# Gate table of a PEER layer from one float32r product a token, with 20 down blocks ahead of the up stage

## The chip, the cores and the metric

One core of one Trainium2 chip runs the whole program. The metric is device time in microseconds, lower is better; the median over several executions is compared.

## What is computed

One transformer block on 256 tokens of width 2048, in float32: an adaptive norm driven by a vector `c` (six vectors of 2048 come out of `silu(c) @ ada_w`), a hybrid mixer (sparse attention beside a gated recurrence), a second adaptive norm, and a PEER feed-forward layer. The sixth vector, `gt2`, scales the feed-forward output at the very end. The change lies in the PEER layer:

```python
def peer_ffn(h, wq, keys, down, up):
    q = (hf @ wq).reshape(T, PEER_HEADS, 2, PEER_DQ // 2)
    s = jnp.einsum('thpd,hpkd->thpk', q, keys)
    v1, i1 = lax.top_k(s[:, :, 0], PEER_TOPK)
    v2, i2 = lax.top_k(s[:, :, 1], PEER_TOPK)
    ...
    cidx = (i1[..., :, None] * PEER_KEYS + i2[..., None, :])
    vals, pick = lax.top_k(cand, PEER_TOPK)
    eidx = jnp.take_along_axis(cidx, pick, axis=-1)
    g = jax.nn.softmax(vals, axis=-1)
    ...
    act = gelu(einsum('td,thkd->thk', x_c, down[e_c])) * g_c
    out = einsum('thk,thkd->td', act, up[e_c])
```

`cand` holds the 256 sums of `v1` and `v2`. There are 16384 experts, and each token picks 8 heads x 16 = 128 of them; the result is scaled by `gt2` and added to `x`.

## The kernel before

The PEER layer is computed densely: all 16384 experts are applied to all 256 tokens, and the activations are multiplied by a table of gates that is zero where an expert wasn't picked. The stages, in order of time:

- **wq** (from 477 us): four blocks of queries and key scores, and the searches for the 16 best (VectorE).
- **down**: 32 down blocks `d` of 512 experts, `gelu(down @ h)` with experts on partitions and tokens along the free axis. `turned` (L376) makes one: eight weight subblocks of 128x1024, 24 matmuls of 256 columns each. The first `LAG` = 14 blocks run ahead of the up stage; their results are stored to `xd` in DRAM and loaded again (`xS`) when they are due.
- **up**: 16 groups of four up blocks `u`, 48 matmuls of 512 columns each, added to `acc` by VectorE. From `LAG` on, a down block runs ahead of every two up blocks (groups 6 to 14); earlier groups hold up blocks alone.

All these products are float32 in three passes: every weight tile `raw` (1 MB, loaded through SP's queue into four buffers, in the order of the list `items`) is split into a high and a low float32r part, `wh` by a ScalarE cast (L206) and `wl` by a VectorE subtraction (L207); `fill` keeps two subblocks ready ahead of TensorE.

The **gate table** needs, for each token, a 128x128 matrix with the gates at the picked pairs of keys. `picks` (L1130, once for each half of the tokens) turns the search results into key indices and gates, transposes them (`pkT`) and copies them to `idT` and `gT` (picks along partitions, tokens along the free axis). `w_build` (L1178) then takes steps of four tokens. In step q VectorE makes the one-hot rows `oh` of both key indices (L1185), ScalarE scales the one-hot rows of the first by the gates of step q-1 (L1206), TensorE multiplies for step q-2 in plain float32 (L1201), and ScalarE copies the product of step q-3 from PSUM into `stg` (L1193); every eight steps POOL's queue stores `stg` to `wd` in DRAM. There are 64 steps. `act` (L1231) later loads the table's part `wt`, multiplies it into the activations and splits them (`ah`, `al`).

Such side work is written as generators. `tick` runs once a weight subblock and advances the first generator in the list of jobs by `RATES[prio]` steps: evictions have priority 0, searches and `act` 1, `picks` 2, `w_build` 3; while `w_build` is at step `WK` or below it goes at the full rate (two steps a subblock in the down stage). So `RATES` and `WK` set how thickly the table's steps lie among the down matmuls. All jobs that are left are run without a pause ahead of the last of the `LAG` blocks. Weight splits have a raised priority in the scheduler, so they are placed ahead of the steps.

The sixth vector's 16 chunks `ada` of 1 MB come in the same list `items`, one behind each up block of groups 4 to 7; VectorE reduces each against `cb` (L228, 128x2048). At the end of group 8 the vector is closed and broadcast into `cb` (`bcast_row`).

Of the kernel before, what the change touches and what calls it, by code (L numbers as in the profile page):

```python
# [7 lines left out]
F32 = mybir.dt.float32  # L8
F32R = mybir.dt.float32r
U32 = mybir.dt.uint32  # L10
I32 = mybir.dt.int32
AF = mybir.ActivationFunctionType
OP = mybir.AluOpType
AX = mybir.AxisListType

P = 128
D = 2048
S = 256
# [9 lines left out]
NE = 16384  # L28
NEB = NE // 512
NUG = NE // 1024  # L30
LAG = 14
RATES = (2, 1.8, 1, 1.1)
WK = 4
RG = 2
CDS = ((0, 1, 16), (1, 4, 8), (4, 16, 4))
NCD = 88
# [9 lines left out]
AHEAD = 2  # L46

TURN, WROOM, XTURN = 24, 1088, 8
LEAD = 50
LEAD2 = 350  # L50
SEGS = (('f', 0, 2), ('a', 0, 4), ('f', 2, 6), ('a', 4, 8))
# [16 lines left out]
def kernel(  # L68
# [24 lines left out]
    V, A, T, G = nc.vector, nc.scalar, nc.tensor, nc.gpsimd  # L93
# [12 lines left out]
    def ps_t(name):  # L106
        return ps[0].tile([P, 512], F32, tag="t", bufs=ps[2], name=name)
# [25 lines left out]
    x1d = dp.tile([NT, P, D], F32, name="x1d")  # L133
    xd = dp.tile([LAG, P, 4, S], F32, name="xd")
    wd = dp.tile([8, P, P, 32], F32, name="wd")


    items = []
# [11 lines left out]
    for ch in STREAM.replace(" ", ""):  # L150
# [6 lines left out]
        else:  # L157
            src, o = wid[ch].pop(0)
# [6 lines left out]
    for j in range(4):  # L165
        for h in range(2):
            add_w(wq[j, h], shift=TURN)
    for e in range(LAG):
        for h in range(2):
            add_w(down[e, h], shift=TURN)  # L170
    for g in range(NUG):
        for o in range(2):
            e = 2 * g + 2 + o
            if LAG <= e < NEB:
                for h in range(2):
                    add_w(down[e, h], shift=TURN)
            for q in range(2):
                add_w(up[g, 2 * o + q])
                if 4 <= g < 8:
                    items.append(("ada", 4 * (g - 4) + 2 * o + q))  # L180

    pos = {"load": 0, "take": 0, "sub": 0, "lead": 0, "end": 0, "n": 0, "adl": 0}
    raws, avs = [], []
# [258 lines left out]
    ea, e0, eq = ExitStack(), ExitStack(), ExitStack()  # L442
# [61 lines left out]
    for which, i0, i1 in SEGS:  # L504
# [11 lines left out]
        if not sums[which]:  # L516
            if which == "f":
                t = [vp.tile([P, 2, NT, 512], F32, tag="av", bufs=ADAB, name=f"part{i}") for i in range(2)]
                sums["f"] = [[t[b // 2][:, b % 2, tb] for tb in range(NT)] for b in range(4)]
            else:  # L520
                t = sqp.tile([P, 4, NT, 512], F32, name="sums")
# [534 lines left out]
    for i in range(8):  # L1056
        t = x1T[:, 2 * i:2 * i + 2]
# [19 lines left out]
    kq = e4.enter_context(tc.tile_pool(name="kq", bufs=1))  # L1077
    idT = kq.tile([P, S, 2], F32, name="idT")
    gT = kq.tile([P, S], F32, name="gT")
# [50 lines left out]
    def picks(tb):  # L1130

        hi = kq.tile([P, 2, PH, TOPK], U32, tag="hi", bufs=1, name=f"hi{tb}")
        hf = kq.tile([P, 2, PH, TOPK], F32, tag="hf", bufs=1, name=f"hf{tb}")
        mf = kq.tile([P, 16, TOPK], F32, tag="mf", bufs=1, name=f"mf{tb}")
        sel = kq.tile([P, 3, PH, TOPK], F32, tag="sel", bufs=1, name=f"sel{tb}")
        V.tensor_copy(mf, mi[:, tb])

        V.tensor_scalar(hi[:, 0], pk[:, tb], 3, None, OP.logical_shift_right)
        V.tensor_scalar(hi[:, 1], pk[:, tb], 2, None, OP.logical_shift_right)
        V.tensor_copy(hf, hi)  # L1140
        ra, rb = hf[:, 0], hf[:, 1]
        V.tensor_scalar(ra, ra, -1.0, 0.0, OP.add, OP.max)
        V.scalar_tensor_tensor(out=ra, in0=rb, scalar=-6.0, in1=ra, op0=OP.add, op1=OP.max)
        ex = sel[:, 2]
        V.tensor_scalar(rb, ra, 8.0, 8.0, OP.mult, OP.add)
        V.scalar_tensor_tensor(out=rb, in0=ra, scalar=16.0, in1=rb, op0=OP.mult, op1=OP.min)
        V.tensor_scalar(ex, ra, 4.0, 24.0, OP.mult, OP.add)
        V.tensor_tensor(rb, rb, ex, OP.min)
        V.tensor_copy(ex, pk[:, tb])
        V.tensor_tensor(rb, ex, rb, OP.subtract)  # L1150
        V.tensor_tensor(ex, vl[:, tb], vl[:, tb, :, 0:1].to_broadcast([P, PH, TOPK]), OP.subtract)
        A.activation(ex, ex, AF.Exp)
        yield
        m4 = mf.rearrange("p (h o) k -> p h o k", o=2)
        hp = PH // 2
        shape = [P, hp, TOPK, TOPK]
        io = iota[:, 0:16].unsqueeze(1).unsqueeze(1).to_broadcast(shape)
        for o in range(2):
            for hh in range(2):
                hs = slice(hp * hh, hp * (hh + 1))  # L1160
                eq = kq.tile(shape, F32, tag="eq", bufs=3, name=f"eq{tb}{o}{hh}")
                V.tensor_tensor(eq, hf[:, o, hs].unsqueeze(3).to_broadcast(shape), io, OP.is_equal)
                V.tensor_tensor(eq, eq, m4[:, hs, o].unsqueeze(2).to_broadcast(shape), OP.mult)
                yield
                V.tensor_reduce(sel[:, o, hs], eq, AX.X, OP.add)
        s8 = kq.tile([P, PH], F32, tag="s8", bufs=1, name=f"s8{tb}")
        V.tensor_reduce(s8, ex, AX.X, OP.add)
        V.reciprocal(s8, s8)
        V.tensor_tensor(ex, ex, s8.unsqueeze(2).to_broadcast([P, PH, TOPK]), OP.mult)
        yield  # L1170
        tp = ps_t(f"pkT{tb}")
        for i in range(3):
            T.transpose(tp[:, i * P:(i + 1) * P], sel[:, i].rearrange("p h k -> p (h k)"), ident)
        yield
        A.copy(idT[:, tbs[tb]].rearrange("p t i -> p i t"), tp[:, 0:2 * P].rearrange("p (i t) -> p i t", i=2))
        A.copy(gT[:, tbs[tb]], tp[:, 2 * P:3 * P])

    def w_build():  # L1178

        stg, ohs, gas, wps = {}, {}, {}, {}  # L1180
        for q in range(64 + 3):
            wn[0] = q
            if q < 64:
                oh = kq.tile([P, 4, 2, P], F32, tag="eq", bufs=3, name=f"oh{q}")
                V.tensor_tensor(oh, iota.unsqueeze(1).unsqueeze(1).to_broadcast([P, 4, 2, P]),  # L1185
                                idT[:, 4 * q:4 * q + 4].unsqueeze(3).to_broadcast([P, 4, 2, P]), OP.is_equal)
                ohs[q] = oh
            if 0 <= q - 3:
                p_, tg = q - 3, (q - 3) // 8
                if p_ % 8 == 0:  # L1190
                    stg[tg] = kq.tile([P, P, 32], F32, tag="stg", bufs=1, name=f"stg{tg}")
                o = (p_ % 8) * 4
                A.copy(stg[tg][:, :, o:o + 4], wps.pop(p_).rearrange("p (k i) -> p i k", k=4))  # L1193
                if p_ % 8 == 7:
                    G.dma_start(wd[tg], stg.pop(tg))
            if 0 <= q - 2 < 64:
                p_ = q - 2
                oh = ohs.pop(p_)
                wps[p_] = (ps_p if p_ % 2 else ps_t)(f"w{p_}")
                for k in range(4):  # L1200
                    T.matmul(wps[p_][:, k * P:(k + 1) * P], oh[:, k, 1], oh[:, k, 0], start=True, stop=True)  # L1201
            if 0 <= q - 1 < 64:
                p_ = q - 1
                for k in range(4):
                    t = 4 * p_ + k
                    A.activation(ohs[p_][:, k, 0], ohs[p_][:, k, 0], AF.Copy, scale=gT[:, t:t + 1])  # L1206
            yield


# [85 lines left out]
    for g in range(NUG):  # L1295
        for o in range(2):
# [7 lines left out]
            for q in range(2 * o, 2 * o + 2):  # L1304
# [10 lines left out]
                if q % 2 == 0 and LAG <= eb < NEB:  # L1315
                    finish(0)
                    add(act(eb, upp), 1)
        if g == NUG // 2:
            ada_close(5, 0, NDC)
            add(bcast_row(cb, 5), 1)  # L1320
        if g < NUG - 1:
# [96 lines left out]
```

## Time and profile before

| what | value |
|---|---|
| median of three runs | 2052.03 us (2051.98 to 2058.9) |
| profiled execution, device time | 2056.6 us |
| its span, first to last instruction | 2054.8 us |
| TensorE matmul busy | 1979.6 us (96%) |
| VectorE busy | 1451.0 us (71%) |
| ScalarE busy | 1016.1 us (49%) |
| DMA | 509.12 MB, 248 GB/s mean |

The profile is of one execution. Busy time is the union of an engine's instructions; TensorE's matmuls overlap one another in the records, so the time from one start to the next, and not a record's length, is what a matmul costs. PEld is TensorE's weight load, which runs beside the matmuls. A table of stretches gives start:end and length in us, then for each engine its busy us and the count of its instructions, then TensorE's granted clock (1.00 is full speed), the busy share of the DMA engines and GB/s. A group names the source line, the engine and the tiles as output<-inputs; a releaser is what ended an engine's idle time.

### The profile page before, as it was taken

To read this page: it belongs to the slowest core of one execution; us is meant where nothing else is said; L and a number is where in the kernel's file an instruction comes from. 1 tells how busy PE (TensorE), PEld (TensorE's weight loads), DVE (VectorE), ACT (ScalarE), POOL (GpSimd) and SP (SyncE) were. 2 spreads that over 40 slices of the span, in tenths; PEclk is the share of its full clock that TensorE was granted. 3 is DMA by queue.
4 is the path that set the end of the run, shared out by engine and by line. 5 is a ranking of instruction groups with operands and counts; after the bars stand their busy time and mean duration, and the time that the engine had idled before them with its cause. 6 is when DMAs were issued, how large, how long until landed. Compare 5 with 4: busy or idle time off the path is not lost.

```text
span 2054.8 us, 31264 instructions
## 1 busy us (share of the span) xinstructions
PE 1979.6 (96%) x12602; PEld 1751.4 (85%) x12602; DVE 1451.0 (71%) x2149; ACT 1016.1 (49%) x1454; POOL 61.0 (3%) x95
## 2 busy tenths in 40 slices
PE   5999998998999999999999999999999999999998
PEld 4777565788999999998888789899999889999997
DVE  7888999887999666546667766665555555555566
ACT  2544676455446988645444334444444444444442
POOL 0000000000000000001000000000000000000000
PEclk8999998898999999999999999999999999999999
DMA  9898778995455666778767777776555666556663
GB/s 361 333 361 337 273 302 326 343 342 207 165 179 192 227 244 244 253 262 308 256 232 259 270 263 258 256 265 209 197 199 200 214 203 208 202 203 207 198 226 130
DMA packets 75873, 509.12 MB, mean 248 GB/s; under 512 B 8528, under 2 KB 9040, under 8 KB 20176
## 3 DMA queue, kind: packets, MB, share of 16 engines
q1 hardware_dynamic: 63792, 450.50, 60.7%
q0 software_dynamic: 11936, 56.63, 8.2%
q8 instruction: 98, 1.61, 0.3%
q14 instruction: 47, 0.39, 0.1%
HBM read 478.78 MB, written 28.31 MB: 247 GB/s over the span
## 4 chain that ended last, share of the span: by engine, by line
PE 64%; issue 16%; DVE 12%; DMA 4%; ACT 2%; POOL 1%; DVEq 0%; SPq 0%; POOLq 0%; ACTq 0%
PE d L374 8%; PE d L373 8%; PE d L372 8%; PE u L356 7%; PE u L355 7%; PE u L357 7%; DVE wl L207 3%; DVE av L228 3%; DMA raw<-in_ada_w_dram 2%; PE wq L372 2%; PE wq L373 2%; PE wq L374 2%; PE y L357 1%; PE y L355 1%; PE y L356 1%
## 5 line engine op out<-in xcount | busy, mean ns | idle before, releaser
L207 DVE TENSOR_TENSOR wl<-raw,wh 128x1024 fp32r<-128x1024 f32 x649 | 788.9, 1221 | 462.8 <-ACT wh L206 460.0
L206 ACT CAST wh<-raw 128x1024 fp32r<-128x1024 f32 x649 | 679.9, 1050 | 808.7 <-PE u L357 374.2
L372 PE MATMUL d<-xH,wh 128*128 128x256 f32 x2048 | 571.4, 279 | 0.0
L374 PE MATMUL d<-xH,wl 128*128 128x256 f32 x2048 | 568.0, 277 | 0.8 <-DVE wl L207 0.7
L373 PE MATMUL d<-xL,wh 128*128 128x256 f32 x2048 | 567.6, 277 | 0.0
L356 PE MATMUL u<-wl,ah 128*128 128x512 f32 x1024 | 400.0, 391 | 4.2 <-DVE wl L207 4.2
L355 PE MATMUL u<-wh,ah 128*128 128x512 f32 x1024 | 398.9, 390 | 0.0
L357 PE MATMUL u<-wh,al 128*128 128x512 f32 x1024 | 398.6, 389 | 0.0
L374 PEld LDWEIGHTS d<-xH,wl 128*128 128x128 f32 x2048 | 384.9, 188 | 1.3 <-DVE wl L207 1.2
L372 PEld LDWEIGHTS d<-xH,wh 128*128 128x128 f32 x2048 | 385.2, 188 | 0.7
L373 PEld LDWEIGHTS d<-xL,wh 128*128 128x128 f32 x2048 | 384.9, 188 | 0.7
L356 PEld LDWEIGHTS u<-wl,ah 128*128 128x128 f32 x1024 | 192.2, 188 | 46.4 <-DVE wl L207 7.4
L357 PEld LDWEIGHTS u<-wh,al 128*128 128x128 f32 x1024 | 192.4, 188 | 40.2
L355 PEld LDWEIGHTS u<-wh,ah 128*128 128x128 f32 x1024 | 192.2, 188 | 39.7
L228 DVE SCALAR_TENSOR_TENSOR av<-av,cb 128x2048 f32<-128x2048 f32 x64 | 145.8, 2283 | 6.2 <-DMA av<-in_ada_w_dram 6.2
L1185 DVE TENSOR_TENSOR oh<-con,idT 128x1024 f32<-128x1024 f32 x64 | 78.0, 1223 | 58.4 <-PE w L1201 58.4
L1206 ACT ACTIVATE oh<-oh,gT 128x128 f32<-128x128 f32 x256 | 83.1, 396 | 24.9 <-DVE oh L1185 24.9
L372 PE MATMUL wq<-xH,wh 128*128 128x256 f32 x256 | 73.5, 288 | 2.5 <-ACT xH L206 2.5
L373 PE MATMUL wq<-xL,wh 128*128 128x256 f32 x256 | 73.2, 286 | 0.0
L374 PE MATMUL wq<-xH,wl 128*128 128x256 f32 x256 | 73.0, 285 | 0.0
L1262 DVE TENSOR_TENSOR acc<-acc,u 128x512 f32<-128x512 f32 x112 | 71.5, 679 | 0.0
L1201 PE MATMUL w<-oh 128*128 128x128 f32 x512 | 69.8, 276 | 0.2 <-ACT stg L1193 0.2
(359 smaller groups left out, 2007.9 us busy)
## 6 DMA issues: line engine op xcount, KB each, us to landing
raw<-in_down_dram SPq DMA_DIRECT2D x128, 1024.0 KB, 5.2
raw<-in_up_dram SPq DMA_DIRECT2D x128, 1024.0 KB, 5.1
av<-in_ada_w_dram SPq DMA_DIRECT2D x64, 1024.0 KB, 7.0
raw<-in_w_a_dram SPq DMA_DIRECT2D x32, 1024.0 KB, 9.0
raw<-in_ada_p_dram SPq DMA_DIRECT2D x16, 1024.0 KB, 7.1
raw<-in_w_out_dram SPq DMA_DIRECT2D x16, 1024.0 KB, 7.9
raw<-in_wq_dram SPq DMA_DIRECT2D x16, 1024.0 KB, 5.2
wd<-stg POOLq DMA_DIRECT2D x8, 2048.0 KB, 8.0
```

What stands on the lines that cost most here:

```text
L206: A.copy(dst_h, src)
L207: V.tensor_tensor(dst_l, src, dst_h.bitcast(F32), OP.subtract)
L228: V.scalar_tensor_tensor(out=t, in0=t, scalar=1.0, in1=cb, op0=OP.mult, op1=OP.mult, accum_out=m)
L355: T.matmul(o, ah, bh, start=first, stop=False)
L356: T.matmul(o, ah, bl, start=False, stop=False)
L357: T.matmul(o, al, bh, start=False, stop=last)
L372: T.matmul(o, wh[:, kk, ws], bH[:, kc], start=f and i % 2 == 0, stop=False)
L373: T.matmul(o, wh[:, kk, ws], bL[:, kc], start=False, stop=False)
L374: T.matmul(o, wl[:, kk, ws], bH[:, kc], start=False, stop=e and i % 2 == 1)
L1185: V.tensor_tensor(oh, iota.unsqueeze(1).unsqueeze(1).to_broadcast([P, 4, 2, P]), idT[:, 4 * q:4 * q + 4].unsqueeze(3).to_broadcast([P, 4, ...
L1206: A.activation(ohs[p_][:, k, 0], ohs[p_][:, k, 0], AF.Copy, scale=gT[:, t:t + 1])
L1262: V.tensor_tensor(a, a, pst[tb], OP.add)
```

## The change

- The table's product: the gate `gT` is split once into `gh` (float32r) and `gl` (the rest). In each step VectorE makes the one-hots as float32r, ScalarE writes the first one-hot times `gh` and VectorE the first one-hot times `gl` into a new tile `ga`, and one float32r matmul of 256 columns per token gives both parts. The two parts go to two PSUM tiles of two tokens each; ScalarE copies the high part to `stg` and VectorE adds the low part. The pipeline of steps is one longer (product for step q-3, copies for step q-4).
- `oh` and `ga` get tags of their own with three buffers each, `ga` with an offset of 48 elements inside its tile (`GPLACE`); the tag `eq` remains with `picks`.
- `LAG` 14 to 20: 20 down blocks ahead of the up stage; 20 stores and loads of `xd`; groups 0 to 8 hold up blocks alone, 9 to 14 have the down blocks.
- `RATES` for `picks` 1 to 0.7, for `w_build` 1.1 to 0.51; `WK` 4 to 0. `picks` gets one more empty step ahead of its transposes.
- The sixth vector's chunks move from groups 4 to 7 into groups 9 to 12, its end from group 8 to 13.

```diff
@@ -28,9 +28,10 @@
 NE = 16384
 NEB = NE // 512
 NUG = NE // 1024
-LAG = 14
-RATES = (2, 1.8, 1, 1.1)
-WK = 4
+LAG = 20
+RATES = (2, 1.8, 0.7, 0.51)
+WK = 0
+ADG = 9
 RG = 2
 CDS = ((0, 1, 16), (1, 4, 8), (4, 16, 4))
 NCD = 88
@@ -46,6 +47,8 @@
 AHEAD = 2
 
 TURN, WROOM, XTURN = 24, 1088, 8
+
+GPLACE = 48
 LEAD = 50
 LEAD2 = 350
 SEGS = (('f', 0, 2), ('a', 0, 4), ('f', 2, 6), ('a', 4, 8))
@@ -176,8 +179,8 @@
                     add_w(down[e, h], shift=TURN)
             for q in range(2):
                 add_w(up[g, 2 * o + q])
-                if 4 <= g < 8:
-                    items.append(("ada", 4 * (g - 4) + 2 * o + q))
+                if ADG <= g < ADG + 4:
+                    items.append(("ada", 4 * (g - ADG) + 2 * o + q))
 
     pos = {"load": 0, "take": 0, "sub": 0, "lead": 0, "end": 0, "n": 0, "adl": 0}
     raws, avs = [], []
@@ -1168,6 +1171,7 @@
         V.reciprocal(s8, s8)
         V.tensor_tensor(ex, ex, s8.unsqueeze(2).to_broadcast([P, PH, TOPK]), OP.mult)
         yield
+        yield
         tp = ps_t(f"pkT{tb}")
         for i in range(3):
             T.transpose(tp[:, i * P:(i + 1) * P], sel[:, i].rearrange("p h k -> p (h k)"), ident)
@@ -1175,35 +1179,53 @@
         A.copy(idT[:, tbs[tb]].rearrange("p t i -> p i t"), tp[:, 0:2 * P].rearrange("p (i t) -> p i t", i=2))
         A.copy(gT[:, tbs[tb]], tp[:, 2 * P:3 * P])
 
+    def turn_tile(tag, place, dt, name):
+
+        t = kq.tile([P, 4 * 2 * P + (64 if place else 0)], dt, tag=tag, bufs=3, name=name)
+        return t[:, place:place + 4 * 2 * P].rearrange("p (k o i) -> p k o i", k=4, o=2)
+
     def w_build():
 
         stg, ohs, gas, wps = {}, {}, {}, {}
-        for q in range(64 + 3):
+        gl = kq.tile([P, S], F32, name="gl")
+        gh = kq.tile([P, S], F32R, name="gh")
+        A.copy(gh, gT)
+        V.tensor_tensor(gl, gT, gh.bitcast(F32), OP.subtract)
+        for q in range(64 + 4):
             wn[0] = q
             if q < 64:
-                oh = kq.tile([P, 4, 2, P], F32, tag="eq", bufs=3, name=f"oh{q}")
+                oh = turn_tile("oh", 0, F32R, f"oh{q}")
                 V.tensor_tensor(oh, iota.unsqueeze(1).unsqueeze(1).to_broadcast([P, 4, 2, P]),
                                 idT[:, 4 * q:4 * q + 4].unsqueeze(3).to_broadcast([P, 4, 2, P]), OP.is_equal)
                 ohs[q] = oh
-            if 0 <= q - 3:
-                p_, tg = q - 3, (q - 3) // 8
+            if 0 <= q - 4:
+                p_, tg = q - 4, (q - 4) // 8
                 if p_ % 8 == 0:
                     stg[tg] = kq.tile([P, P, 32], F32, tag="stg", bufs=1, name=f"stg{tg}")
                 o = (p_ % 8) * 4
-                A.copy(stg[tg][:, :, o:o + 4], wps.pop(p_).rearrange("p (k i) -> p i k", k=4))
+                for k, w in enumerate(wps.pop(p_)):
+                    w4 = w.rearrange("p (k o i) -> p i o k", k=2, o=2)
+                    d = stg[tg][:, :, o + 2 * k:o + 2 * k + 2]
+                    A.copy(d, w4[:, :, 0])
+                    V.tensor_tensor(d, d, w4[:, :, 1], OP.add)
                 if p_ % 8 == 7:
                     G.dma_start(wd[tg], stg.pop(tg))
-            if 0 <= q - 2 < 64:
-                p_ = q - 2
-                oh = ohs.pop(p_)
-                wps[p_] = (ps_p if p_ % 2 else ps_t)(f"w{p_}")
+            if 0 <= q - 3 < 64:
+                p_ = q - 3
+                oh, ga = ohs.pop(p_), gas.pop(p_)
+                wps[p_] = [ps_t(f"w{p_}0"), (ps_p if p_ % 2 else ps_t)(f"w{p_}1")]
                 for k in range(4):
-                    T.matmul(wps[p_][:, k * P:(k + 1) * P], oh[:, k, 1], oh[:, k, 0], start=True, stop=True)
+                    T.matmul(wps[p_][k // 2][:, k % 2 * S:k % 2 * S + S], oh[:, k, 1], ga[:, k].rearrange("p o i -> p (o i)"),
+                             start=True, stop=True)
             if 0 <= q - 1 < 64:
                 p_ = q - 1
+                ga = turn_tile("ga", GPLACE, F32R, f"ga{p_}")
+                gas[p_] = ga
+                hot = ohs[p_][:, :, 0].bitcast(F32)
+                V.tensor_tensor(ga[:, :, 1], hot, gl[:, 4 * p_:4 * p_ + 4].unsqueeze(2).to_broadcast([P, 4, P]), OP.mult)
                 for k in range(4):
                     t = 4 * p_ + k
-                    A.activation(ohs[p_][:, k, 0], ohs[p_][:, k, 0], AF.Copy, scale=gT[:, t:t + 1])
+                    A.activation(ga[:, k, 0], hot[:, k], AF.Copy, scale=gh[:, t:t + 1].bitcast(F32))
             yield
 
 
@@ -1315,7 +1337,7 @@
                 if q % 2 == 0 and LAG <= eb < NEB:
                     finish(0)
                     add(act(eb, upp), 1)
-        if g == NUG // 2:
+        if g == ADG + 4:
             ada_close(5, 0, NDC)
             add(bcast_row(cb, 5), 1)
         if g < NUG - 1:
```

## Rows read from the trace of the kernel before

**Rows 1.** The page: engines' busy us, share, instructions; TensorE's busy tenths in 40 slices.
```profile
PE 1979.6 (96%) x12602; PEld 1751.4 (85%) x12602; DVE 1451.0 (71%) x2149; ACT 1016.1 (49%) x1454; POOL 61.0 (3%) x95
PE   5999998998999999999999999999999999999998
```

**Rows 2.** Stretches: length; busy us (x count) of PE, PEld, DVE, ACT, POOL; PEclk; DMA.
```profile
576.20:949.50 373.30, 368.26 (x3218) 366.23 (x3217) 260.86 (x345) 248.02 (x474) 18.05 (x31) 1.00 0.65 234
599.00:626.00 27.00, 23.17 (x196) 22.24 (x195) 26.93 (x39) 12.15 (x14) 0.54 (x1) 1.00 0.56 193
715.50:834.50 119.00, 119.00 (x1052) 119.00 (x1050) 78.61 (x67) 96.58 (x213) 4.78 (x9) 1.00 0.65 239
862.40:949.50 87.10, 87.10 (x771) 87.10 (x770) 44.07 (x42) 39.85 (x43) 9.00 (x14) 1.00 0.79 279
526.30:550.70 24.40, 24.40 (x210) 24.40 (x210) 23.35 (x112) 10.57 (x13) 0.00 (x0) 1.00 0.50 172
576.20:655.00 78.80, 73.99 (x638) 72.46 (x636) 78.57 (x187) 38.16 (x47) 1.61 (x3) 1.00 0.56 194
```

**Rows 3.** Stretches, instructions on tile `d` alone: PE, PEld, ACT; PEclk; DMA.
```profile
715.50:834.50 119.00, 95.58 (x769) 90.05 (x769) 4.98 (x9) 1.00 0.65 239
862.40:949.50 87.10, 87.10 (x770) 87.02 (x768) 4.80 (x9) 1.00 0.79 279
```

**Rows 4.** Table of stretches in the up stage; columns as in rows 2.
```profile
1005.80:1136.40 130.60, 130.60 (x578) 108.15 (x576) 88.59 (x102) 56.37 (x54) 8.02 (x11) 1.00 0.71 242
1136.40:1217.10 80.70, 78.06 (x337) 62.54 (x336) 59.42 (x60) 31.39 (x30) 0.00 (x0) 1.00 0.79 287
1217.10:1304.40 87.30, 87.30 (x578) 79.68 (x577) 57.49 (x59) 37.72 (x38) 1.76 (x2) 1.00 0.72 253
1391.60:1435.20 43.60, 43.60 (x289) 39.82 (x288) 24.54 (x26) 18.85 (x19) 0.88 (x1) 1.00 0.61 205
```

**Rows 5.** Stretches, instructions on tile `w` alone: PE, PEld, ACT; PEclk; DMA.
```profile
576.20:949.50 373.30, 69.78 (x512) 63.89 (x512) 36.10 (x64) 1.00 0.65 234
715.50:834.50 119.00, 36.44 (x283) 33.94 (x281) 19.25 (x34) 1.00 0.65 239
```

**Rows 6.** Waits of TensorE, 576 to 949 us: total us, times, longest.
```profile
PE pkT L1173 <- DVE sel L1165: 4.0, 4, 1.8
```

**Rows 7.** Groups by line, 1136.4 to 1217.1 us: busy, mean ns, idle before, releaser.
```profile
L228 DVE SCALAR_TENSOR_TENSOR raw<-raw,cb 128x2048 f32<-128x2048 f32 x6 | 13.8, 2292 | 14.7 <-DMA raw<-in_ada_w_dram 14.7
...
L356 PE MATMUL u<-wl,ah 128*128 128x512 f32 x112 | 44.4, 397 | 2.6 <-DVE wl L207 2.6
```

**Rows 8.** Groups by line over the span; columns as in rows 7.
```profile
L207 DVE TENSOR_TENSOR wl<-raw,wh 128x1024 fp32r<-128x1024 f32 x649 | 788.9, 1221 | 462.8 <-ACT wh L206 460.0 <-PE a L357 2.2
L206 ACT CAST wh<-raw 128x1024 fp32r<-128x1024 f32 x649 | 679.9, 1050 | 808.7 <-PE u L357 374.2 <-PE d L373 290.7 <-PE wq L373 46.5
L1185 DVE TENSOR_TENSOR oh<-con,idT 128x1024 f32<-128x1024 f32 x64 | 78.0, 1223 | 58.4 <-PE w L1201 58.4
L1206 ACT ACTIVATE oh<-oh,gT 128x128 f32<-128x128 f32 x256 | 83.1, 396 | 24.9 <-DVE oh L1185 24.9
L1193 ACT COPY stg<-w 128x512 f32<-128x512 f32 x64 | 36.1, 584 | 4.2 <-DMA wd<-stg 3.0 <-PE w L1201 1.1
L1215 ACT ACTIVATE xT<-d 128x512 f32<-128x512 f32 x64 | 38.0, 593 | 28.4 <-PE d L374 28.4
L1262 DVE TENSOR_TENSOR acc<-acc,u 128x512 f32<-128x512 f32 x112 | 71.5, 679 | 0.0
L1311 DVE TENSOR_TENSOR acc<-acc,xr 128x512 f32<-128x512 f32 x8 | 5.5, 683 | 0.0
L1238 DVE TENSOR_TENSOR xT<-xT,wt 128x256 f32<-128x256 f32 x72 | 27.3, 420 | 8.6 <-ACT xT L1215 8.6
L800 DVE SCALAR_TENSOR_TENSOR pt<-sc,rq,con 128x256 f32<-128x256 f32 x16 | 7.4, 476 | 0.0
```

**Rows 9.** Groups of VectorE by line, 576.2 to 655 us; columns as in rows 7.
```profile
L207 DVE TENSOR_TENSOR wl<-raw,wh 128x1024 fp32r<-128x1024 f32 x27 | 32.5, 1212 | 0.0
```

## The prediction

> **What bounds the kernel now.** I read the page first: TensorE is busy 96% of the span, VectorE, the next, 71% [rows 1]. A busy share alone doesn't say that TensorE runs at its pace, so the second view is a table of stretches with edges at the starts of blocks (a block is the 192 matmuls of one `turned` call or the 48 of one `up_block`). Four clean down blocks take 87.1 us for 770 matmuls, so 21.78 us a block and 113.1 ns a matmul [rows 2, 3]; twelve clean up blocks take 130.6 us, 10.88 us each [rows 4]. [...] So from the down stage on, the time is a count of matmul columns plus the places where a block is longer than its clean length. Those places are what the change touches:
> - The 14 down blocks ahead of the up stage take 373.3 us, and 14 clean ones would take 304.9: 68.4 us over [rows 2].
> - The gate table's products stand in this stage: 512 instructions (two for each of 256 tokens) [rows 5]. In the steady part, 119.0 us hold four down blocks (769 matmuls) and 283 table instructions [rows 2, 3, 5]. 119.0 - 87.1 = 31.9 us for 283 is 112.7 ns each, 0.90 us for a step of four tokens, 57.7 us for all 64 steps. No cover: TensorE is busy for all 119.0 us and nothing waits, so each of these us is on the path.
> - 18 other matmuls of the stage (3218 - 14 x 192 - 512 [rows 2, 5]) are some 2.0 us at the same 113 ns. 68.4 - 57.7 - 2.0 = 8.7 us are true stalls. They lie in the second to fourth block; in the second, the longest but for the table's, VectorE is busy 26.93 of 27.0 us [rows 2] and TensorE waits for `sel` of `picks`, 4.0 us in four waits [rows 6]; part of the rest is weights that came late behind the same work.
> - In the up stage, 80.7 us hold seven up blocks, 76.2 at the clean length: 4.5 us lost [rows 4]. These are the blocks in which the chunks of the sixth vector (1 MB each) are loaded beside weights while no down block runs; VectorE sits 14.7 us waiting for such chunks and TensorE 2.6 us for VectorE's splits behind them [rows 7].
>
> **The table's product.** Now: float32, 128 columns, two instructions, 57.7 us. After: one float32r product of 256 columns with a 128x128 stationary operand, the very shape of the down matmul. 256 x 113.1 ns = 29.0 us. The same shape in the wq blocks costs more: 24.40 us for 192 of it and 18 others [rows 2], (24.40 - 18 x 0.113) / 192 = 116.5 ns, which would make 29.8 us. I take 29.0, since the table's products will stand among the down matmuls. Term: -28.7 us (-27.9 at the dearer pitch). [...]
>
> **What it adds on VectorE and ScalarE.** Prices are of one instruction [rows 8]. VectorE per step: the one-hot table stays at 1.22 us; new are a product of 512 elements (0.68, as the adds of 512) and two adds of 256 out of PSUM. For these 0.42 us is the nearest row in kind (a two-input product of 256), 0.476 the nearest with a PSUM source. So 2.74 to 2.85 us in place of 1.22; I take 2.74. ScalarE: four scalings are unchanged, one copy of 512 (0.58) becomes two of 256, between 0.29 (half) and 0.58 (no shorter) each, so 0 to 0.58 us more. Once: a 256-wide copy and subtraction, below 1 us.
> Following the ticks by hand: `picks` ends in the second eighth of down block 3 (counted from 0), the table runs from the fourth eighth of block 3 to the sixth of block 17, some 114 weight subblocks. VectorE's work there: 114 x 1.221 = 139.2 (splits) and 64 x 2.74 = 175.4, together 314.6 us. TensorE's: 14.25 x 21.78 + 29.0 = 339.4 us. So VectorE fills 93%, with 24.8 us or 0.39 us a step to spare (0.28 at the upper price). ScalarE: 114 x 1.05 + 28 x 0.59 + 64 x (83.1 / 64 = 1.30 for four scalings and 0.58 to 1.17) = 257 to 294 us, 87% at most. At the old rate of some nine steps a block VectorE would need 9.8 + 9 x 2.74 = 34.4 us beside 21.8 + 9 x 0.453 = 25.9 us of TensorE; at the new 4 to 5 it fits. That is the cover for the 97 us (64 x 1.52) that VectorE gains, and if it goes, the excess is on the path.
> The wq blocks show such a cover holding: VectorE busy 23.35 of 24.40 us, 96%, and TensorE busy all of it [rows 2]. `picks` shows it failing at 99.7%. Between them, at 93% with uneven steps (4 or 5 a block, now and then two close together), I put **+4 us** of stalls; bounds 0 and 29 (below).
>
> **Waits that it adds.** The one-hot tile of step q takes the buffer of step q-3, whose product is now emitted in the same step and not in the step before. VectorE already waits there, 58.4 us for 64 steps [rows 8], with nothing lost on TensorE. Behind the waiting instruction are the splits of the next weights, for which TensorE waits; two subblocks (5.4 us) lie ready ahead. Each add waits for a ScalarE copy; behind it stand the same splits. The `stg` tile still has one buffer: the first copy of each eight steps waits for the store to `wd` behind POOL's queue. These transfers, six more stores and loads of `xd` among them, move through POOL's queue, where the gelu's third buffer gives them two blocks of time. No term.
>
> **Picks.** Same VectorE work, 78.57 us busy in 78.8 less 32.5 of splits and 2.4 of one-hot, so 43.7 us of search and picks (two one-hots at 1.22) [rows 2, 9]. Now its last piece falls due in the middle of block 2; after, in block 3, with one more step between the last sums and the transposes that wait for them. By the transposes' new place (576.2 + 3.1 x 21.78 + 1.5 = 645) VectorE owes 43.7 + 26 x 1.22 = 75.4 us of 69: still 6 us short, part of which the extra step and the table's own lead (products stand three steps behind the one-hots) can absorb. Left between 0 and 8.7 us; I take 5, so **-3.7 us**.
>
> **Down blocks and chunks moved.** Six down blocks change place; in the mixed groups one down and two up blocks take 43.6 us [rows 4], the sum of their clean lengths is 43.54: nothing. The sixth vector's 16 chunks pass, in SP's queue, from up-only groups into groups 9 to 12, where each pair of up blocks has a down block beside it. Groups of that mixed kind that carried chunks took 87.3 us for two pairs (one of two such groups stands), against 43.6 for one without [rows 4]: no loss. The weights that now load earlier by those places only gain time. Term **-4.5 us**, bounds -4.5 and 0. The broadcast of that vector moves with it at its own cost.
>
> **Sum.** -28.7 - 3.7 - 4.5 + 4 = -33 us. The profiled execution took 2056.6 us, so 2023.6 for one like it; the median of the runs shown is 2052.0, 4.6 below it, so I predict **2019 us**.
>
> **Rivals.**
> 1. All of it hides: no stall from VectorE, `picks` clean: 2052.0 - 28.7 - 8.7 - 4.5 = 2010. For: 93%. Against: uneven steps, VectorE owing 6 us at the start of the table.
> 2. VectorE becomes the bound: an add of 256 out of PSUM into a strided tile costs twice the row. 64 x 0.84 = 54 us more, less 25 to spare, 29 on the path in place of 4: 2044. For: no row has VectorE reading and writing such strides. Against: the ScalarE copy with the same strides took its usual 0.58 us. [...]
> 3. **Slower**: the in-order waits don't overlap. If VectorE stands at each one-hot for the product of the same step as long as now (58.4 / 64 = 0.91 us) and at each add for its copy (0.29 to 0.58), 1.5 to 2.1 us a step, 64 x 1.8 - 25 = 90 us come on the path: 2052 - 37 + 90 = 2105. It turns slower by over 0.5% from (37 + 25 + 10) / 64 = 1.1 us of wait a step. For: ScalarE is some 80% busy, and its casts stand between the copies. Against: a wait for TensorE shrinks as VectorE falls behind, and now it costs nothing.
> 4. The change doesn't do what it says: the float32r product takes as long as the float32 pair. 2052 - 3.7 - 4.5 + 0 = 2044. Against: the same shape runs at 113 ns beside it.
>
> **How the numbers follow.** A measurement of this kernel can tell 0.5%, 10 us, from no change. Forecast with its stalls of 0 to 15 us (2012 to 2031): 0.54. Rival 1: 0.15. Rival 2, from 2031 to 2050: 0.19, half of it below 2042. Rival 4: 0.03. Rival 3: 0.09, of it 0.01 within 0.5%. Faster: 0.54 + 0.15 + 0.10 = 0.79; same: 0.09 + 0.03 + 0.01 = 0.13; slower 0.08. The range for 8 in 10 runs from rival 1 with 2 us to spare, 2008, to 2042.
>
> **What would show it.** Right: 256 records of the table's product at the down matmul's length; a down block with 4 or 5 steps at 23.6 to 24.0 us; VectorE at 90 to 95% there; groups 4 and 5 at 10.88 us a block; no loss in groups 9 to 12. Wrong: TensorE idle before `d` or the product, released by VectorE's splits or adds, above 10 us in sum; an add above 0.6 us; down blocks above 25 us; VectorE idle for ScalarE's copies by over 1 us a step.

## The result, and the profile after

Measured beside one another, the kernel before has a median of 2053.0 us and the changed one 2027.6 us (2027.1 to 2029.0): a ratio of 0.987, with its interval from 0.985 to 0.989. The forecast was 2019 with a range of 2008 to 2042, so the time lies inside it, 8.6 us above the point. The profiled execution of the changed kernel took 2027.1 us, with a span of 2025.3; its lines have moved (casts and splits of weights L209 and L210, the table's one-hots L1198, scaling L1228, product L1218, copies L1209, adds L1210).

Engines' busy time and TensorE's tenths, from the page, for [rows 1]:

```profile
PE 1953.6 (96%) x12346; PEld 1728.4 (85%) x12346; DVE 1529.3 (76%) x2342; ACT 1024.1 (51%) x1519; POOL 67.6 (3%) x107
...
PE   5999898898999999999999999999999999999998
```

256 instructions of TensorE are gone (12602 to 12346), 26 us of its busy time with them, and VectorE has 78 us more. The stretches, with the columns of [rows 2]; the first is the whole down stage with its 20 blocks:

```profile
574.70:1057.10 482.40, 475.45 (x4113) 473.66 (x4112) 398.19 (x586) 312.56 (x599) 21.24 (x37) 1.00 0.68 240
664.50:1002.60 338.10, 335.58 (x2897) 335.00 (x2896) 280.47 (x358) 241.00 (x509) 11.18 (x21) 1.00 0.67 237
660.00:757.00 97.00, 97.00 (x859) 97.00 (x858) 81.40 (x102) 69.30 (x145) 3.20 (x6) 1.00 0.67 237
760.00:935.00 175.00, 173.08 (x1467) 172.90 (x1468) 144.34 (x184) 123.33 (x261) 5.85 (x11) 1.00 0.67 237
1013.60:1057.10 43.50, 43.50 (x386) 43.50 (x385) 24.47 (x26) 20.85 (x23) 7.92 (x12) 1.00 0.92 339
1102.30:1232.90 130.60, 130.60 (x578) 108.18 (x577) 87.57 (x103) 56.40 (x55) 8.71 (x12) 1.00 0.72 241
1276.40:1385.20 108.80, 108.80 (x482) 90.12 (x481) 72.93 (x86) 46.92 (x45) 6.71 (x9) 1.00 0.71 237
1450.50:1799.40 348.90, 348.90 (x2305) 318.54 (x2304) 229.68 (x234) 150.86 (x152) 7.07 (x8) 1.00 0.74 253
```

- The up stage is clean in these stretches (its third block takes 12.48 us, 12.77 before). Twelve up blocks take 130.60 us, as in [rows 4]; the last row holds all 16 chunks beside eight down and sixteen up blocks and takes 348.9 us, where eight times the clean 43.6 makes 348.8.
- The down stage takes 482.4 us. Less six blocks of 21.78 this is 351.7, against 373.3 for the same 14 blocks and the table before [rows 2]: 21.6 us won.
- Of two stretches of the same make (down blocks with four or five table steps each) the first runs at 97.00 / 859 = 112.9 ns a matmul and the second, by its busy time, at 173.08 / 1467 = 118.0. The clock is 1.00 in both. From start to start in the records it is 113.3 ns until the gap at 759.6 us, 117.8 from there to 937, and 113.35 again. This is the part of the result that the prediction had no term for.

The same on the tile `w` alone, PE, PEld, DVE, ACT, for [rows 5]:

```profile
576.00:1057.00 481.00, 40.62 (x256) 34.43 (x256) 48.26 (x128) 43.61 (x128) 1.00 0.68 241
```

Waits of TensorE in the down stage (total us, times, longest), for [rows 6]:

```profile
PE w L1218 <- DVE stg L1210: 2.5, 3, 1.4
PE pkT L1177 <- DVE sel L1172: 2.2, 2, 1.1
PE pkT L1177 <- DVE sel L1168: 1.4, 1, 1.4
PE d L377 <- DVE wl L210: 0.7, 1, 0.7
```

Groups by line in the down stage, for [rows 8]:

```profile
L210 DVE TENSOR_TENSOR wl<-raw,wh 128x1024 fp32r<-128x1024 f32 x161 | 196.2, 1220 | 40.0 <-ACT wh L209 38.8
...
L1228 ACT ACTIVATE ga<-oh,gh 128x128 fp32r<-128x128 f32 x256 | 83.0, 394 | 18.1 <-DVE oh L1198 16.3
L1198 DVE TENSOR_TENSOR oh<-con,idT 128x1024 fp32r<-128x1024 f32 x64 | 78.1, 1221 | 33.4 <-PE w L1218 33.3
L1210 DVE TENSOR_TENSOR stg<-stg,w 128x256 f32<-128x256 f32 x128 | 48.3, 421 | 10.3 <-ACT stg L1209 10.3
L1225 DVE TENSOR_TENSOR ga<-oh,gl 128x512 fp32r<-128x512 f32 x64 | 43.6, 683 | 0.0
L1209 ACT COPY stg<-w 128x256 f32<-128x256 f32 x128 | 43.6, 400 | 11.6 <-DMA wd<-stg 11.6
L1218 PE MATMUL w<-ga,oh 128*128 128x256 f32 x256 | 40.6, 280 | 2.5 <-DVE stg L1210 2.5
```

The new wait of the table is read along its idle column, from L1209 upwards: ScalarE stands 11.6 us for the store of `stg`, VectorE's adds 10.3 us for ScalarE's copies, and TensorE 2.5 us for the buffer that an add has not yet emptied. One such place, in order of time (start, us, engine and line; idle time before it and its releaser), on ScalarE:

```profile
759.49 0.94 ACT L1209 COPY stg<-w 128x256 f32<-128x256 f32 x3 [2.77 <-DMA wd<-stg]
760.29 1.07 ACT L209 CAST wh<-raw 128x1024 fp32r<-128x1024 f32 x1
```

and on VectorE:

```profile
756.75 0.68 DVE L1225 TENSOR_TENSOR ga<-oh,gl 128x512 fp32r<-128x512 f32 x1
759.91 1.08 DVE L1210 TENSOR_TENSOR stg<-stg,w 128x256 f32<-128x256 f32 x3 [2.48 <-ACT stg L1209]
761.39 1.22 DVE L210 TENSOR_TENSOR wl<-raw,wh 128x1024 fp32r<-128x1024 f32 x1 [0.40 <-ACT wh L209]
```

The `wd` store issued at 748.7 us lets ScalarE go at 759.5. TensorE's stream breaks here (0.9 us from one start to the next), and it is from this break that the matmuls run at 117.8 ns.

### The profile page after: what moved, and what is told of

The parts are those of the page before. It is cut to its first block, busy times and chain, and to the rows that moved or that the text cites. A ratio compares the mean times of both kernels' runs of the same rounds, so it can differ in the third digit from the quotient of the medians.

```text
span 2025.3 us, 30935 instructions
## 1 busy us (share of the span) xinstructions
PE 1953.6 (96%) x12346; PEld 1728.4 (85%) x12346; DVE 1529.3 (76%) x2342; ACT 1024.1 (51%) x1519; POOL 67.6 (3%) x107
## 4 chain that ended last, share of the span: by engine, by line
PE 75%; DVE 10%; issue 10%; DMA 3%; ACT 2%; POOL 1%; SPq 0%; DVEq 0%; POOLq 0%
PE u L359 11%; PE u L358 11%; PE u L360 11%; PE d L377 8%; PE d L376 8%; PE d L375 8%; DVE av L231 3%; DVE wl L210 3%; PE wq L375 2%; PE wq L376 2%; PE wq L377 2%; PE y L360 1%; PE y L358 1%; PE y L359 1%; DMA wd<-stg 1%
## 5 line engine op out<-in xcount | busy, mean ns | idle before, releaser
L210 DVE TENSOR_TENSOR wl<-raw,wh 128x1024 fp32r<-128x1024 f32 x649 | 789.3, 1220 | 374.7 <-ACT wh L209 372.0
L209 ACT CAST wh<-raw 128x1024 fp32r<-128x1024 f32 x649 | 680.2, 1051 | 768.5 <-PE u L360 364.2
L1198 DVE TENSOR_TENSOR oh<-con,idT 128x1024 fp32r<-128x1024 f32 x64 | 78.1, 1221 | 33.4 <-PE w L1218 33.3
L1228 ACT ACTIVATE ga<-oh,gh 128x128 fp32r<-128x128 f32 x256 | 83.0, 394 | 18.1 <-DVE oh L1198 16.3
L1210 DVE TENSOR_TENSOR stg<-stg,w 128x256 f32<-128x256 f32 x128 | 48.3, 421 | 10.3 <-ACT stg L1209 10.3
```

The costliest lines, as they stand in the source:

```text
L209: A.copy(dst_h, src)
L210: V.tensor_tensor(dst_l, src, dst_h.bitcast(F32), OP.subtract)
L1228: A.activation(ga[:, k, 0], hot[:, k], AF.Copy, scale=gh[:, t:t + 1].bitcast(F32))
```

## The experiments

Three questions: which part of the change earns what, what the 117.8 ns come from, and whether a better version follows.

**The parts, one at a time.** The product alone, with `LAG`, rates, `WK`, chunks and the `picks` step as before:

```diff
-LAG = 20
-RATES = (2, 1.8, 0.7, 0.51)
-WK = 0
-ADG = 9
+LAG = 14
+RATES = (2, 1.8, 1, 1.1)
+WK = 4
+ADG = 4
...
-        yield
```

> The new product alone: 14 blocks ahead, the old rates (picks 1, table 1.1, full rate up to step 4), one empty step fewer in picks, the sixth vector's chunks in groups 4 to 7. Theory (VectorE has no room at the old rate): per block some nine steps ask VectorE for 9.8 + 9 x 2.74 = 34.4 us beside 25.8 us of TensorE, so the table stage lasts as long as VectorE's 64 x 2.74 + its splits, some 245 us where it was 213: 20 to 35 us slower than the kernel before, 2073 to 2088 us. Rival (the splits' priority and the three steps of slack absorb it): the product's gain comes through at the old rate as well, 2053 - 29 + 5 = 2029 us.

Measured: 2065.1 us, ratio 1.0051 (1.0035 to 1.0068): slower than before, if less than expected. Two down blocks with nine steps and two with eight to ten, in stretches as above:

```profile
728.10:861.20 133.10, 119.63 (x914) 115.28 (x913) 121.99 (x173) 100.07 (x254) 4.27 (x8) 0.94 0.56 214
```

and TensorE's waits in the table stage:

```profile
PE d L377 <- DVE wl L210: 12.5, 11, 2.5
PE w L1217 <- DVE stg L1209: 5.5, 9, 1.7
```

The four blocks take 33.3 us each (34.4 worked out from VectorE's durations). TensorE idles 13.5 us, released by VectorE, and the clock falls to 0.94 in a stretch where it was 1.00 before. But VectorE too idles, 11 us: no engine is full, they wait for one another in order. The 0.94 is a mean: in four spells, 17.1 us in all, each of which began during a stop of 1.5 to 2.7 us or within 1.5 us of its end, the granted clock is 0.50, the lower of the two levels in the records (1 - 0.5 x 17.1 / 133.1 makes the 0.94). There 69 matmuls take 213 ns from start to start in place of 113 to 118, some 7 us of TensorE's time; how much of it adds to the 10.7 was not separated. So the thin rates are what makes the product pay. The expected times overshot because from the first product to the last the table takes 240 us here and 203 before, but holds 7.8 down blocks in place of 6.6: some 27 of these 37 us are blocks that have to run anyway.

Everything but the product, the float32 pair kept. One place of the product against the changed kernel; the one-hots, scalings and copies of the table are the old ones too:

```diff
-                    T.matmul(wps[p_][k // 2][:, k % 2 * S:k % 2 * S + S], oh[:, k, 1], ga[:, k].rearrange("p o i -> p (o i)"),
-                             start=True, stop=True)
+                    T.matmul(wps[p_][:, k * P:(k + 1) * P], oh[:, k, 1], oh[:, k, 0], start=True, stop=True)
```

> All of the change but the product: the old float32 product with its two instructions, 20 blocks ahead, the new rates, the extra step in picks, the chunks in groups 9 to 12. Theory: the product is worth 28.7 us, the rest of the change some 7 to 9 us (picks 3.6, chunks 4.5), so 2053 - 8 = 2045 us, and no slow stretch as long as no gap opens. Rival (the spreading out is what gained, by leaving VectorE room): most of the 25 us are here, 2032 us or less.

Measured: 2047.9 us, ratio 0.9966 (0.9953 to 0.9978). The sum's terms for `picks` and chunks make -8.2 us, and -6.5 came. Where the table now ends just ahead of the up stage, the second and third up block take 11.84 and 16.29 us, against 10.88 and 12.77 before: 4.5 us lost there. The two parts alone give +10.7 and -6.5 us, together -25.4: the gain is in the pair.

The changed kernel with its chunks back in groups 4 to 7, where with `LAG` 20 all are up-only:

```diff
-ADG = 9
+ADG = 4
```

> The changed kernel with the sixth vector's chunks in groups 4 to 7 again, which now hold up blocks alone. Theory: chunks beside up blocks alone cost 4.5 us for the seven blocks after the start of group 4 in the kernel before; here all four groups are of that kind, so 4.5 to 10 us more: 2032 to 2038 us. Rival (the loss of the kernel before came from the late start of weight loads behind the table, not from the chunks): within 1 us of 2027.6.

Measured: 2046.2 us, ratio 0.9955 (0.9938 to 0.9971), 18.6 us above the changed kernel, far more than expected. Sixteen up blocks with chunks:

```profile
1232.60:1427.10 194.50, 179.58 (x769) 142.75 (x768) 146.25 (x164) 74.98 (x72) 9.64 (x13) 1.00 0.82 295
```

Their waits, on VectorE and on TensorE:

```profile
DVE raw L231 <- DMA raw<-in_ada_w_dram: 36.3, 14, 4.1
```

```profile
PE u L359 <- DVE wl L210: 14.9, 15, 1.6
```

Sixteen clean blocks take 174.1 us, so 20.4 are lost, 1.3 a chunk, where eight chunks before cost 4.5 us or 0.6 each [rows 4, 7]. The DMA share is 0.82 in place of 0.72, VectorE stands for chunks and TensorE behind it for splits. Moving the chunks is therefore not a separate gain of 4.5 us: it belongs to `LAG` 20, which takes 18.6 us more without it.

`picks` at its old rate and without the added step, the rest as changed:

```diff
-RATES = (2, 1.8, 0.7, 0.51)
+RATES = (2, 1.8, 1, 0.51)
...
-        yield
```

> The changed kernel with the picks stage as before: one step a subblock in place of 0.7 and one empty step fewer ahead of its transposes. Theory: TensorE's waits for picks were 5 us in the changed kernel and 8.7 before, so 3 to 4 us more, 2031 us, give or take what the pace behind the gaps makes (up to 4 us in the blocks next to them). Rival (the table's later start is what costs): the earlier start leaves more room and the time is the same or less, 2025 to 2028 us.

Measured: 2037.4 us (2028.9 to 2039.5), ratio 0.9908 (0.9882 to 0.9935). The waits for `sel` are back at 4.0 us in four, as in [rows 6]. The rest is not `picks`: the profiled execution (2039.5) waits 7.1 us for `stg` and runs some 270 us at 117.8 ns, against 191 in the changed kernel.

**The buffer behind the gaps.** Theory: the one `stg` buffer makes the table's gaps, and the gaps make the slow pace. Rival: the pace has its own cause, and two buffers only save 3 us. To make room, the four one-hots of `picks` share a tile with the second buffer:

```diff
-    kt = kq.tile([P, 16, P], F32, tag="stg", bufs=1, name="kt")
+    kt = kq.tile([P, 16, P], F32, tag="stg", bufs=2, name="kt")
+    eqb = kq.tile([P, 4, 1024], F32, tag="stg", bufs=2, name="eqb")
...
-                eq = kq.tile(shape, F32, tag="eq", bufs=3, name=f"eq{tb}{o}{hh}")
+                eq = eqb[:, 2 * o + hh].rearrange("p (h a b) -> p h a b", h=hp, a=TOPK)
...
-                    stg[tg] = kq.tile([P, P, 32], F32, tag="stg", bufs=1, name=f"stg{tg}")
+                    stg[tg] = kq.tile([P, P, 32], F32, tag="stg", bufs=2, name=f"stg{tg}")
```

> The changed kernel with a second buffer for the staging tile stg (its space comes from the tile of the picks stage, which is done by then), so that ScalarE's copy for the next eight steps no longer waits until the store to wd has landed. Theory (gaps): in the changed kernel TensorE waited 2.5 us in three gaps for the low-part add behind that copy, and between the first and the last of these gaps (759 to 937 us) every 256-column matmul took 117.8 ns in place of 113.4, 6.6 us more. Without the gaps both go: 2027.6 - 9 = 2018 to 2020 us, all matmuls from 660 us on at 113.4 ns. Rival (load or place): the slow pace comes from the table's own traffic or the place of its tiles; then the gaps go (2.5 us) but the slow stretch stays: 2025 us.

Measured: 2015.8 us (2014.2 to 2017.7), ratio 0.9815 (0.9799 to 0.9832). It is the fastest kernel of this study, below both others. TensorE no longer waits for `stg`, and the pace holds from 621 us to the end of the stage:

```profile
621.00:1043.00 422.00, 420.81 (x3711) 420.57 (x3712) 347.88 (x435) 289.83 (x572) 20.23 (x35) 1.00 0.71 253
498.30:545.40 47.10, 47.10 (x418) 47.10 (x417) 44.20 (x209) 21.04 (x25) 0.00 (x0) 1.00 0.51 172
```

420.81 / 3711 = 113.4 ns, and every down block with four or five steps takes 23.57 or 24.03 us. The second row is two blocks of wq, 23.59 each and not the 24.40 of [rows 2]: the dearer pitch there is no property of that stage either. A record's length tells the paces apart. The table's product (duration in ns min/median/max) after, and in this kernel:

```profile
L1218 PE MATMUL w<-ga,oh x256: 276/281/361, 664.5 to 1002.6; 128*128 128x256 f32 x128
```

```profile
L1219 PE MATMUL w<-ga,oh x256: 276/276/276, 660.5 to 988.6; 128*128 128x256 f32 x128
```

The same with more empty steps ahead of the transposes of `picks`, four `yield`s in place of two, and then three:

```diff
         yield
+        yield
+        yield
         tp = ps_t(f"pkT{tb}")
```

> The kernel with two staging buffers (2015.8 us), and two more empty steps in picks, so four in all, ahead of its transposes. Theory: VectorE owes some 6 us when the transposes fall due; two steps more are 7.8 us, so the waits of 1.9, 1.4 and 1.4 us that are left go, and the table still ends ahead of the last of the 20 blocks: 2011 to 2013 us. Rival (VectorE's debt only moves on into the table's steps): new waits of TensorE for the splits appear in the blocks behind, and the time stays within 1 us of 2015.8.

> Two staging buffers, and one more empty step in picks ahead of its transposes, three in all (four made the table end too late: 4.2 and 2.7 us of waits at the start of the up stage). Theory: half of the 4.5 us of waits for picks goes and the table still ends in time: 2013 to 2015 us, if the table stage keeps the 113.4 ns pace. Rival: what the step saves comes back at the start of the up stage, 2016 to 2020 us.

Measured: 2020.0 us (2018.7 to 2038.1) with four, ratio 0.9834 (0.9818 to 0.985), and 2016.8 (2014.6 to 2019.6) with three, 0.9832 (0.9816 to 0.9849). Neither gains on the kernel with two buffers alone. The gaps of `picks` go, but the table ends later, and the loss comes back at the start of the up stage: the third up block takes 17.23 and 15.41 us, against 12.48 after. With three, this is what TensorE waits for:

```profile
PE d L377 <- DVE wl L210: 4.4, 5, 1.7
PE u L359 <- DVE wl L210: 2.7, 3, 2.0
```

The profiled execution of the one with four took 2038.1 us, and shows a whole table stage at the other pace. Its stretch, and then its products:

```profile
636.00:1053.00 417.00, 413.45 (x3504) 412.82 (x3504) 329.80 (x415) 280.32 (x560) 18.16 (x32) 1.00 0.68 239
```

```profile
L1221 PE MATMUL w<-ga,oh x256: 280/281/282, 677.2 to 1021.0; 128*128 128x256 f32 x128
```

3504 matmuls at 117.8 in place of 113.3 ns are 15.6 us, most of the 18 between this execution and the median. The pace began behind a gap of 0.3 us at 636 us and ended at 1053, 3.6 us behind a gap of 2.9 us; between them (one more gap of 1.2 us at 644.5, then none for 400 us) down blocks without any gap take 24.97 and 24.50 us. So a gap doesn't cost its length alone: the pace behind it can stay for hundreds of us, here 417.

The second buffer also moves other tiles in memory, and that is not separated from the gaps in these runs. Places alone don't explain the quick pace, though: the kernel with four steps has every tile at the place of the one with two, and ran its table stage at the slow one.

**What sets the pace.** Theory: the pace depends on where the operands lie and is taken up at a break of the stream. Rival: a gap has nothing to do with it, or the places have not. The offset of `ga` first:

```diff
-GPLACE = 48
+GPLACE = 0
```

> The changed kernel with the product tile ga at offset 0 of its buffer (GPLACE 0 in place of 48). Theory (gaps, not places): the products keep the pace of the down matmuls around them, 113.4 or 117.8 ns, and the time is 2027.6 within 4 us, as long stretches fall to the one pace or the other. Rival (the place matters): the products alone are slower than the down matmuls beside them, from 10 ns each (2.6 us in all) to double (29 us).

Measured: 2031.8 us (2026.7 to 2037.6), ratio 0.9894 (0.9866 to 0.9921). In the records the pace now changes at nearly every table step, with no gap: 113.5 ns for 47 matmuls, 117.8 for 57, and so on. Two stretches, one of each:

```profile
734.60:739.80 5.20, 5.20 (x49) 5.20 (x48) 4.79 (x6) 3.36 (x8) 0.00 (x0) 1.00 0.40 117
739.90:746.50 6.60, 6.60 (x59) 6.60 (x57) 4.85 (x6) 5.29 (x11) 0.53 (x1) 1.00 0.61 212
```

With the offset of 48, steps don't change the pace in the profiles above (113.4 ns over 422 us with two `stg` buffers). The step itself can be the break, if its operands lie so (113.5 to 117.8 ns here, with `ga` at offset 0).

Breaks made on purpose: ahead of each down block of the up stage, VectorE rewrites one column of `xH` with its own value, after the last up block's product is there. TensorE must stop. In the first form the saved column is a new tile:

```diff
+    sv = bp.tile([P, 1], F32, name="sv")
+    V.tensor_copy(sv, xH[:, 0, 0:1].bitcast(F32))
...
                 if eb >= LAG:
+                    V.scalar_tensor_tensor(out=xH[:, 0, 0:1], in0=last[0][:, 0:1], scalar=0.0, in1=sv, op0=OP.mult, op1=OP.add)
...
-                    add(ev_u(g, q, up_block(g, q)), 0)
+                    last = up_block(g, q)
+                    add(ev_u(g, q, last), 0)
```

> The changed kernel with a forced stop of TensorE ahead of each of the 12 down blocks of the mixed groups: VectorE rewrites one column of the high part of the input (with the value that it has) once the last up block's product is there, so the down block's first matmul waits for VectorE. In the changed kernel these 12 blocks and the up blocks behind them run at 113.4 ns per 256 columns without exception, no table is built there and VectorE is 60% busy. Theory (a gap decides the pace of what follows): after some of the 12 gaps, though not all, the 256-column matmuls run at 117.8 ns, and they keep that pace until the next gap or other break. Rival (the pace is one of the table stage's traffic): all 12 blocks at 113.4 ns, and only the gaps themselves are lost, 12 x 0.3 to 1.5 us.

Measured: 2068.6 us, one run. It can't be read as meant: even ahead of the first stop all up blocks take 11.20 us and not 10.88. The new tile had moved others. So the tile was added alone, without a stop:

> The changed kernel with a tile of one column (4 bytes a partition) allocated and written once ahead of the feed-forward stage, and nothing else; the tiles allocated behind it move in memory, ah and al of the up stage among them. In the run with the forced stops such a tile stood there too, and all 64 up blocks took 11.20 us in place of 10.88, also those ahead of the first stop. Theory (the place of the operands sets the pace too): all up blocks at 11.2 us, some 20 us more in all. Rival (the stops did it): up blocks at 10.88 us, the time within 5 us of 2027.6.

Measured: 2065.4 us, one run. Ten up blocks, to be set beside the 108.80 us of the same 482 matmuls after:

```profile
1268.50:1380.50 112.00, 112.00 (x482) 90.33 (x481) 71.71 (x82) 46.92 (x46) 6.37 (x9) 1.00 0.67 230
```

All clean up blocks run so, and the clean down blocks take 22.62 us: 38 us above the changed kernel, for one column of 4 bytes. In the kernel with stops, which has the same tile, no product of the table is shorter than 280 ns, the length at the slower pace; five of its six blocks behind a gap took 21.86 us, the sixth 22.69 and those without a gap 22.62: there a break restored the quicker pace.

The stops again, with the saved column in the unused end of the `xL` tile, so that nothing moves (the other lines as above):

```diff
+    sv = xHL[1][:, NDC * S + 40:NDC * S + 41].bitcast(F32)
+    V.tensor_copy(xHL[1][:, NDC * S + 40:NDC * S + 41], xH[:, 0, 0:1].bitcast(F32))
```

> The forced stops ahead of the 12 down blocks of the mixed groups once more, with the saved column in the unused end of the low part of the input, so that no tile moves. Theory (a gap can change the pace, an unbroken stream keeps it): up blocks ahead of the first stop at 10.88 us; behind a stop that opens a gap the down block is at one of two lengths, 21.8 or 22.6 us, and keeps its pace until the next break. Rival (with the places of the changed kernel nothing but 113.4 ns is to be had): all 12 at 21.8 us and the gaps.

Measured: 2034.3 us, one run. Up blocks are at 10.88 us. Six stops opened gaps, which lengthen the up block ahead of them to 12.08. Down blocks on the tile `d` alone (PE, PEld, ACT), the first, third and fifth behind a gap, the second and fourth not:

```profile
1450.60:1473.30 22.70, 22.70 (x192) 22.65 (x192) 0.52 (x1) 1.00 0.59 215
1495.10:1516.90 21.80, 21.80 (x192) 21.78 (x192) 0.46 (x1) 1.00 0.63 218
1539.90:1561.80 21.90, 21.86 (x192) 21.85 (x192) 0.48 (x1) 1.00 0.61 215
1583.60:1605.50 21.90, 21.87 (x192) 21.84 (x192) 0.50 (x1) 1.00 0.63 227
1628.50:1651.20 22.70, 22.70 (x192) 22.65 (x192) 0.52 (x1) 1.00 0.61 214
```

Three of the six blocks behind a gap take 22.69 us from start to start, three 21.86; no block without a gap is slow, though VectorE rewrote the column ahead of these too, and the up blocks that follow are back at 10.88. So a gap can bring the slow pace, and doesn't always: here it does so at every second one. What decides it stays open.

The places of all d operands, last: with two `stg` buffers as above, the weights of wq and down and `xH`, `xL` at offset 0 in their tiles.

```diff
-TURN, WROOM, XTURN = 24, 1088, 8
+TURN, WROOM, XTURN = 0, 1088, 0
```

> Two staging buffers, and the weights and the input of the down stage at offset 0 of their tiles (24 and 8 elements before). Theory (the place of the operands sets the pace): the down blocks no longer hold 113.4 ns even in unbroken stretches; clean ones take 22.6 us or more, from 27 us more in all. Rival (only gaps decide): down blocks at 21.8 us and 2016 us.

Measured: 2060.3 us, one run. Two clean down blocks, to be set beside the 43.50 us after:

```profile
1030.00:1076.10 46.10, 46.10 (x387) 46.10 (x386) 24.47 (x26) 20.88 (x23) 7.46 (x12) 1.00 0.88 313
```

Every clean down block of the kernel takes 23.03 us, 120 ns a matmul, and the up blocks, whose operands stayed, 10.88. A third pace of the same instruction, with nothing else changed than these places; the kernel with two buffers holds 113.4 ns.

## Why the prediction was right, and where it was off

- **The product, -28.7 us: right.** 256 records at the down matmul's length (280 ns in the mean, 278 for `d`), and blocks with four or five steps at 23.57 and 24.03 us as long as the pace is 113.3 ns: (23.57 - 21.76) / 16 = 113 ns. Eight of the thirteen blocks from 671 to 990 us, at the other pace or with a gap, are longer (24.50 to 26.17), and three of them pass the 25 us that the prediction had as a sign of being wrong. The product was not slower than the shape beside it (rival 4).
- **VectorE's and ScalarE's additions: right in size.** 1.22 + 0.68 + 2 x 0.42 = 2.75 us a step, 2.74 predicted. The add out of PSUM takes 421 ns, the product in SBUF of the same size 420 [rows 8]: rival 2 fell. ScalarE's copy takes 400 ns, between its ends of 290 and 580.
- **VectorE at 90 to 95%: wrong, too high.** In the table's 338.1 us it is busy 280.5, 83%. The records of neighbouring instructions overlap by some 83 ns: their durations sum up to 303.5 us (90%), and 23 of those are counted twice. The sum of durations was no bound of the engine. The cover was thicker than I had it.
- **Stalls of +4 us: right in size by luck.** Breaks in the table's steps cost 3.0 us. They came from `stg`, to which the text gave "No term", and not from VectorE's thin cover. The in-order waits of rival 3 stayed hidden: 33.3 us for the one-hots' buffers and 10.3 for copies, 0.7 a step, below the 1.1 from which it would have turned.
- **Picks, -3.7: right.** The breaks from the second to the fourth block cost 5.3 us, 5 predicted, 8.7 before.
- **Chunks, -4.5: right** as a difference of these two kernels; run alone against the old place it was 18.6 (above).
- **One pace for a shape: the mis-sized term.** The sum took 113.1 ns for every matmul of the stage. 1477 matmuls at 117.8 and 153 more at the start cost (1477 + 153) x 4.4 ns = 7.2 us. The rows to see it by were there: the wq blocks at 116.5 [rows 2], which I read as a price of their place in the kernel (from start to start in the records they are at 117.8). With two `stg` buffers the same blocks ran at 113.3, so it is no price of that place.
- **From the profile to the median.** The sum for a profiled execution was 2023.6, and 2027.1 came: +7.2 for the pace, -1.0 for the stalls, +0.3 for `picks`, -1.9 in pieces under 1 us of the up stage, and -1.5 ahead of the down stage, +3.1 of 3.5. To this I took off 4.6 us because before's profiled execution was slower than the median. The changed kernel's is not (0.5 below its own), and this offset was the larger half of the miss: 3.5 + 4.6 + 0.5 = 8.6.

The down stage by itself adds up: -28.7 - 3.4 + 3.0 + 7.2 = -21.9, against the 21.6 won.

## What to carry to other kernels

A side job that is fed into a TensorE-bound stream must leave no gap in it: look for single buffers behind a store, also where the wait on the engine itself is short, since a break of 0.9 us was followed by 177 us at a pace 4% slower, and one of 0.3 us by 417. A faster instruction is worth its saving only with the rates that spread its helpers (the product alone, at the old rates, took 2065.1 us, 10.7 more than before), and a load that is moved is priced against the place where it will lie (18.6 us more in groups 4 to 7 with `LAG` 20), not the one that it left (4.5). Work out a shape's pitch from several stretches, and where they differ, carry both into the sum.

## What the runs showed of the hardware

- One float32r matmul of 256 columns ran at 113.3, 117.8 or 120 ns at a granted clock of 1.00; places of its operands (two clean down blocks in 43.50 or 46.10 us) and breaks in the stream (21.86 or 22.69 us for the block behind a stop) both changed which. The records of the table's product are 276 ns long at the first pace and 281 at the second. The up stage's 512 columns took 226.7 ns (10.88 us for 48) or 233.3 (11.20).
- An unbroken stream of down blocks and table steps kept its pace, for 400 us in one case. The pace was seen to change at gaps, once 3.6 us behind one, at table steps with their operand at offset 0 (113.5 to 117.8 ns), and at the hand-over between down and up blocks (down blocks of 22.69 us, up blocks of 10.88 behind them).
- Executions of one kernel with several gaps differ by up to 19 us (2018.7 to 2038.1). In the slowest, which is the one with a profile, the slow pace is worth 15.6 us; of the others no trace exists.
- Which pace a stream takes up behind a gap was not settled, nor why the places matter. The runs with stops, with the added column and with all d operands at offset 0 are of one execution each.
